# A two-layer decoder trunk on one core: norm and first queries ahead of the values' products, scores with turned sign, two heads' scores in the two halves of the array's rows

## The chip, the core and the metric

The kernel runs on one core of a Trainium2 chip. The time is that of one execution on the device, in microseconds (us). The core has a matrix engine (TensorE, 128 x 128, which multiplies a stationary operand loaded beforehand with a moving one), VectorE, ScalarE, GpSimd, and SyncE (SP), which here only issues DMAs. Every engine works through a queue of its own in order and waits at semaphores for the others. Products land in eight PSUM banks of 128 x 512 floats, which GpSimd can't read.

## What is computed

A trunk of two layers on 512 tokens of width 1024 in float32: a causal pooling mixer with a gated MLP, then sliding-window attention with a gated MLP, and a final norm. The change concerns the attention alone (16 heads of width 64, 4 key/value heads, window 128):

```python
hn = rms_norm(h, norm_mix[i])
qkv = hn @ w_qkv + b_qkv
# blocks of 128 queries against the previous and their own block of keys
scores = einsum('bnqkgd,bnskd->bnkgqs', q, kb) * HEAD_DIM ** -0.5
scores = where(mask, scores - slopes * dist, -inf)
m = maximum(max(scores, axis=-1), sink)
p = exp(scores - m)
denom = sum(p, axis=-1) + exp(sink - m)
o = einsum('bnkgqs,bnskd->bnqkgd', p / denom, vb)
h = h + o @ w_o
```

## The kernel before

Every large product is made of three: each float32 operand is split into a high part (fp32r, written by ScalarE) and a low part (the remainder, a subtraction on VectorE or GpSimd), and `mm3` (lines 82 to 86) adds high x high, high x low and low x high in one bank. `weights` (93 to 100) fetches a 512 KB tile of weights over SP into one of three raw buffers and splits it into one of four pairs of buffers; a fifth tile waits until the first is used up.

Ahead of the attention the last MLP product adds into the residual `h`, and `after0` (367) splits `h` scaled by the norm's weights into `xs1` and adds up the squares on GpSimd. The norm's factor itself is applied to the products afterwards: `stats` (226) sums the squares over the features with eight narrow products and makes the reciprocal root of 4 numbers per partition with 13 small VectorE operations, `spread` (235) turns it into a 128 x 512 tile `rb`.

The attention (lines 382 to 621) runs:

- *Head* (410 to 474): products of the two key tiles (weights 0 and 1), of the values (96 products of 256 columns), `stats`, the product of the first query tile (weights 2), `spread`. Then the key tiles are scaled and get their bias (`ku`), `keys(0)` splits the first key head, `queries(0, ...)` the first two query heads, and the values are evacuated and split into `vh`, `vl`. A key head is kept twice, in the upper and the lower 64 rows, and a query head has its high part in one half of the rows and its low part in the other, so that one full-height product gives high x high plus low x high, and a second one gives the two products with the low part of the keys.
- *Units* (593 to 613): 4 key heads x 4 query blocks. Unit i issues its scores, unit i-2 is transposed, unit i-3 is weighted with the values. `scores` (525) makes eight products of 256 columns, adds slope and distance and takes the maximum on VectorE, turns its sign (`neg`), forms the sinks' term `es`, takes the exponentials with row sums on ScalarE, and scales with the reciprocal of the sum on GpSimd. Between these steps `fill` puts products of the remaining queries (8 steps of three products for each of 7 tiles) and of the output weights, at `RATE` steps a unit, after 16 steps ahead of unit 0.
- *Tail* (614 to 621): the remaining output products and the addition into `h`.

The tile `q` has 8 buffers, two for each of four query tiles. The banks of the scores are a ring `s` of three, those of the projections a ring `pj` of two. The order of instructions on each engine is made by a planner from the program's order and its own estimates of durations; a product may be put between those of another step where it expects a wait.

Of the kernel before, what the change touches and what calls it, by code (L numbers as in the profile page):

```python
# [19 lines left out]
F32 = mybir.dt.float32  # L20
# [3 lines left out]
ALU = mybir.AluOpType  # L24
# [33 lines left out]
def trunk(ctx: ExitStack, tc: tile.TileContext, x_tok, x_t, vecs, w_pool, w_kq, w_v, w_o, w_in, w_out, out_a, out_b):  # L58
# [18 lines left out]
    def bank(tag):  # L77
        rings[tag].append(rings[tag].pop(0))
        return banks[rings[tag][-1]]
# [303 lines left out]
    with tc.tile_pool(name="ap", bufs=2) as ap:  # L383
# [18 lines left out]

        def proj(i, ps, ks=range(NC), w=None):
            w = w or weights(w_kq[i], D, f"kq{i}", G)
            for k in ks:
                mm3(ps, part(w, k), xs1[k], k == 0, k == NC - 1)
            return w


        qps = bank("pj")  # L410
        vps = [bank("s") for a in range(2)]
        ssp = bank("av")
        kps = [bank("t") for c in range(2)]
        kw = [weights(w_kq[i], D, f"kq{i}") for i in range(2)]
        wv = [weights(w_v[:, a * 1024 : (a + 1) * 1024], 1024, f"wv{a}") for a in range(2)]
        for k in range(NC):
            for c in range(2):
                proj(c, kps[c], [k], kw[c])
        for j in range(NT):
            for k in range(NC):  # L420
                xk = tuple(t[:, j * P : (j + 1) * P] for t in xs1[k])
                wk = part(wv[k // 4], k % 4, 256)
                mm3(vps[j // 2][:, (j % 2) * 256 : (j % 2 + 1) * 256], xk, wk, k == 0, k == NC - 1)
        r = norm1.stats(ssp)
        proj(2, qps)
        rb = norm1.spread(bank("s"), r)

        ku = []
        for c in range(2):
            u = ap.tile([P, S], F32, name=f"ku{c}", bufs=1)  # L430
            V.tensor_tensor(u, kps[c], rb, ALU.mult)
            V.tensor_scalar(u, u, col(V_BQKV + 8 + c), None, ALU.add)
            ku.append(u)

        def keys(n):

            src = slice((n % 2) * HD, (n % 2 + 1) * HD)
            dst = slice((1 - n % 2) * HD, (2 - n % 2) * HD)
            u = ku[n // 2]
            kh = ap.tile([P, S], F32R, tag="kh", name=f"kh{n}")  # L440
            kl = ap.tile([P, S], F32R, tag="kl", name=f"kl{n}")
            A.activation(kh[src], u[src], AF.Copy)
            V.tensor_tensor(kl[src], u[src], kh[src].bitcast(F32), ALU.subtract)
            A.activation(kh[dst], u[src], AF.Copy)
            V.tensor_copy(kl[dst], kl[src].bitcast(F32))
            return kh, kl

        def queries(c, ps):

            u = sm.tile([P, S], F32, tag="sq", name=f"q{c}_u")  # L450
            V.tensor_tensor(u, ps, rb, ALU.mult)
            A.activation(u, u, AF.Identity, scale=qs[:, c : c + 1], bias=bqs[:, c : c + 1])
            res = []
            for par in range(2):
                src = slice(par * HD, (par + 1) * HD)
                dst = slice((1 - par) * HD, (2 - par) * HD)
                t = ap.tile([P, S], F32R, tag="q", name=f"q{c}_{par}", bufs=8)
                A.activation(t[src], u[src], AF.Copy)
                V.tensor_tensor(t[dst], u[src], t[src].bitcast(F32), ALU.subtract)  # L459
                res.append(t)  # L460
            return res

        key = {0: keys(0)}
        q = {0: queries(0, qps)}
        for j in range(NT):
# [6 lines left out]
            V.tensor_tensor(dl, v4, dh.bitcast(F32), ALU.subtract)  # L472
        oh = ap.tile([P, NC, S], F32R, name="oh", bufs=1)
# [27 lines left out]
        def work():  # L501

            for c in range(1, NC):
                for _ in fill_q(c):
                    yield 0
# [19 lines left out]
        def scores(n, b):  # L525
# [4 lines left out]
            sink = vec[:, V_SINK + 4 * n : V_SINK + 4 * n + 4]  # L530
            kk = max(b - 1, 0) * P
            sc = []
            for pr in range(2):
                ps = bank("s")
                st = ap.tile([P, 2, 2 * P], F32, tag="sc", name=f"sc{n}{b}{pr}", bufs=6)
                for par in range(2):
                    o = ps[:, par * 256 : par * 256 + 256]
                    qt = q[2 * n + pr][par][:, b * P : (b + 1) * P]
                    for x, kt in enumerate(key[n]):
                        T.matmul(o, lhsT=qt, rhs=kt[:, kk : kk + 256], start=x == 0, stop=x == 1)  # L540
                for par in range(2):
# [3 lines left out]
                        in0=ps[:, par * 256 : par * 256 + w],  # L545
                        in1=dist[:, 2 * P - w :],
                        scale=slopes[4 * n + i],
                        scalar=sink[:, i : i + 1],
                        op0=ALU.add,
                        op1=ALU.max,  # L550
# [3 lines left out]
            V.tensor_scalar(neg, neg, -1.0, None, ALU.mult)  # L554
            V.tensor_tensor(es, neg, sink, ALU.add)
            A.activation(es, es, AF.Exp)
            heads = [sc[i // 2][:, i % 2, :w] for i in range(4)]
            for i, t in enumerate(heads):
                A.activation(t, t, AF.Exp, bias=neg[:, i : i + 1], accum_out=den[:, i : i + 1])  # L559
# [34 lines left out]
        RATE = 3.4  # L594
        fill(2 * NC, 0)
        sc, pt = {}, {}
        for i in range(NU + 3):
            base = 2 * NC + i * RATE
            have = max(i - 3, 0) if i < NU else NU
            if i < NU:  # L600
                n, b = units[i]
                if b == 0:
                    fill((2 * n + 1) * NC, 0)
                sc[i] = scores(n, b)
                if b == 2 and n + 1 < NKV:
                    key[n + 1] = keys(n + 1)
# [159 lines left out]
```

## Time and profile before

| | |
|---|---|
| median of 3 runs | 944.49 us (944.37 to 944.62) |
| profiled execution | 944.47 us, of which the span of the core 942.7 us |
| mean granted TensorE clock | 0.993 of full speed |
| busy share of the span: TensorE, VectorE, ScalarE, GpSimd | 97%, 62%, 45%, 15% |
| attention, from its first to its last product | 390.3 to 569.8 us |

The profile is that of one execution. A group of rows gives the line of the program, the engine, the operation with its operands (names of tiles) and shapes; "idle before" is the time an engine stood still ahead of it, with the operation that ended it. A matmul's duration contains the time until its results have left the array, so that back-to-back products overlap; their rate is read from the distance of their starts. `PEld` is the loading of stationary operands, which overlaps the products. `PEclk` is the granted clock of TensorE in a stretch, 1.00 being 2.4 GHz.

### The profile page before, as it was taken

To read this page: it belongs to the slowest core of one execution; us is meant where nothing else is said; L and a number is where in the kernel's file an instruction comes from. 1 tells how busy PE (TensorE), PEld (TensorE's weight loads), DVE (VectorE), ACT (ScalarE), POOL (GpSimd) and SP (SyncE) were. 2 spreads that over 40 slices of the span, in tenths; PEclk is the share of its full clock that TensorE was granted. 3 is DMA by queue.
4 is the path that set the end of the run, shared out by engine and by line. 5 is a ranking of instruction groups with operands and counts; after the bars stand their busy time and mean duration, and the time that the engine had idled before them with its cause. 6 is when DMAs were issued, how large, how long until landed. Compare 5 with 4: busy or idle time off the path is not lost.

```text
span 942.7 us, 11713 instructions
## 1 busy us (share of the span) xinstructions
PE 919.2 (97%) x4419; PEld 773.1 (82%) x4419; DVE 587.2 (62%) x974; ACT 426.5 (45%) x690; POOL 138.9 (15%) x203
## 2 busy tenths in 40 slices
PE   8999999999999999996999999999999999999997
PEld 7788888888888888885888888888888888888886
DVE  5689775336777654338888581897753367776433
ACT  7565443223444434226877561644432234444432
POOL 9600000000000001442654231000000000000023
PEclk9999999999999999998999999999999999999999
DMA  9133322342322233321101041332223332232312
GB/s 331 64 112 112 111 63 79 98 140 92 112 90 84 75 90 109 112 90 67 46 24 46 1 135 45 112 125 98 65 89 94 133 111 91 90 98 63 92 62 90
DMA packets 28855, 88.13 MB, mean 93 GB/s; under 512 B 3200, under 2 KB 4352, under 8 KB 28800
## 3 DMA queue, kind: packets, MB, share of 16 engines
q1 hardware_dynamic: 28800, 87.40, 28.3%
q8 instruction: 34, 0.56, 0.2%
q14 instruction: 21, 0.17, 0.1%
HBM read 85.29 MB, written 2.10 MB: 93 GB/s over the span
## 4 chain that ended last, share of the span: by engine, by line
PE 90%; DVE 5%; ACT 3%; POOL 1%; issue 1%; ACTq 0%; DVEq 0%; POOLq 0%
PE bank L85 29%; PE bank L84 29%; PE bank L86 29%; PE bank L540 1%; DVE q L459 1%; PE bank L571 1%; ACT sc L559 1%; DVE sc L543 1%; ACT px_h L251 0%; DVE tl L575 0%; DVE vl L472 0%; ACT wi_h L98 0%; PE bank L271 0%; DVE f0x_l L252 0%; PE bank L230 0%
## 5 line engine op out<-in xcount | busy, mean ns | idle before, releaser
L224 POOL TENSOR_TENSOR n_acc<-n_acc,n_sq 128x512 f32<-128x512 f32 (+1 forms) x28 | 39.1, 1397 | 714.2 <-ACT n_sq L215 707.7
L98 ACT ACTIVATE wi_h<-wi_raw 128x1024 fp32r<-128x1024 f32 x88 | 93.0, 1061 | 109.3 <-PE bank L85 102.4
L85 PE MATMUL bank<-f0x_l,wi_h 128*128 128x512 f32 x352 | 137.1, 389 | 0.8 <-DVE f0x_l L252 0.8
L84 PE MATMUL bank<-f0x_h,wi_h 128*128 128x512 f32 x352 | 137.3, 390 | 0.0
L84 PE MATMUL bank<-f1x_h,wi_h 128*128 128x512 f32 x352 | 137.1, 390 | 0.0
L84 PE MATMUL bank<-zh,wo_h 128*128 128x512 f32 (+1 forms) x363 | 137.0, 378 | 0.0
L86 PE MATMUL bank<-f0x_h,wi_l 128*128 128x512 f32 x352 | 137.0, 389 | 0.0
L86 PE MATMUL bank<-f1x_h,wi_l 128*128 128x512 f32 x352 | 137.0, 389 | 0.0
L85 PE MATMUL bank<-f1x_l,wi_h 128*128 128x512 f32 x352 | 136.9, 389 | 0.0
L86 PE MATMUL bank<-zh,wo_l 128*128 128x512 f32 (+1 forms) x363 | 136.6, 376 | 0.0
L85 PE MATMUL bank<-zl,wo_h 128*128 128x512 f32 (+1 forms) x363 | 136.6, 376 | 0.0
L99 DVE TENSOR_TENSOR wi_l<-wi_raw,wi_h 128x1024 fp32r<-128x1024 f32 x84 | 102.8, 1225 | 48.8 <-ACT wi_h L98 36.7
L98 ACT ACTIVATE wo_h<-wo_raw 128x768 fp32r<-128x768 f32 (+1 forms) x70 | 57.5, 822 | 124.0 <-PE bank L85 112.1
L313 DVE TENSOR_TENSOR c_u<-bank,n_rb 128x512 f32<-128x512 f32 x88 | 60.1, 688 | 76.2 <-PE bank L86 76.2
L99 DVE TENSOR_TENSOR wo_l<-wo_raw,wo_h 128x768 fp32r<-128x768 f32 (+1 forms) x66 | 60.4, 915 | 54.4 <-ACT wo_h L98 54.2
L86 PEld LDWEIGHTS bank<-zh,wo_l 128*128 128x128 f32 x363 | 68.3, 188 | 12.5
L84 PEld LDWEIGHTS bank<-zh,wo_h 128*128 128x128 f32 x363 | 68.3, 188 | 12.4
L85 PEld LDWEIGHTS bank<-zl,wo_h 128*128 128x128 f32 x363 | 68.3, 188 | 12.3
L85 PEld LDWEIGHTS bank<-f0x_l,wi_h 128*128 128x128 f32 x352 | 66.1, 188 | 14.7 <-DVE f0x_l L252 1.2
L84 PEld LDWEIGHTS bank<-f0x_h,wi_h 128*128 128x128 f32 x352 | 66.1, 188 | 14.2 <-DVE h L305 0.4
L86 PEld LDWEIGHTS bank<-f1x_h,wi_l 128*128 128x128 f32 x352 | 66.1, 188 | 13.9
L316 ACT ACTIVATE c_t<-c_u,vec 128x512 f32<-128x512 f32 x88 | 70.6, 810 | 15.2 <-DVE c_u L313 14.3
(173 smaller groups left out, 1510.6 us busy)
## 6 DMA issues: line engine op xcount, KB each, us to landing
wi_raw<-w_in SPq DMA_DIRECT2D x88, 512.0 KB, 3.2
wo_raw<-w_out SPq DMA_DIRECT2D x31, 384.0 KB, 3.0
wo_raw<-w_out SPq DMA_DIRECT2D x31, 320.0 KB, 2.9
kq_raw<-w_kq SPq DMA_DIRECT2D x10, 512.0 KB, 3.2
wo_raw<-w_o SPq DMA_DIRECT2D x8, 512.0 KB, 3.3
xt<-x_tok SPq DMA_DIRECT2D x4, 512.0 KB, 5.2
h<-x_t SPq DMA_DIRECT2D x8, 256.0 KB, 7.5
wpool_raw<-w_pool SPq DMA_DIRECT2D x2, 512.0 KB, 8.2
```

Of the source, the lines that this page charges most:

```text
L84: T.matmul(ps, lhsT=wh, rhs=xh, start=start, stop=False, **kw)
L85: T.matmul(ps, lhsT=wh, rhs=xl, start=False, stop=False, **kw)
L86: T.matmul(ps, lhsT=wl, rhs=xh, start=False, stop=stop, **kw)
L98: A.activation(h[:, :n], raw[:, :n], AF.Copy)
L99: (eng or V).tensor_tensor(l[:, :n], raw[:, :n], h[:, :n].bitcast(F32), ALU.subtract)
L224: eng.tensor_tensor(self.acc[:, lo:hi], self.acc[:, lo:hi], sq[:, lo:hi], ALU.add)
L313: V.tensor_tensor(u, ps, rb, ALU.mult)
L316: A.activation(t, u, AF.Identity, bias=col(V_CB + layer * 2 * NF + m), scale=cw[2])
L459: V.tensor_tensor(t[dst], u[src], t[src].bitcast(F32), ALU.subtract)
L540: T.matmul(o, lhsT=qt, rhs=kt[:, kk : kk + 256], start=x == 0, stop=x == 1)
L543: V.tensor_tensor_reduce(out=st[:, par, :w], in0=ps[:, par * 256 : par * 256 + w], in1=dist[:, 2 * P - w :], scale=slopes[4 * n + i], scal ...
L559: A.activation(t, t, AF.Exp, bias=neg[:, i : i + 1], accum_out=den[:, i : i + 1])
```

## The change

The order of the head becomes: keys, `stats`, the product of the first queries (its weights are fetched before those of the values), `spread`, the second half of the value weights, the values, then `ku`, keys, first queries, and, before the values are evacuated, the product of the second queries. The low part of query weights 2 and 3 is made by VectorE instead of GpSimd.

`keys` now splits a whole tile with two key heads once, and four DMAs make a copy with the halves exchanged (`ksh`, `ksl`). `queries` keeps high and low part in two full tiles (three buffers each). `scores` multiplies with the 64 rows of one head alone: for each of two heads in the upper and the lower rows three products, alternating between the halves, each half with a bank of its own. The scores come out with the opposite sign of the bias, so that a minimum gives `neg` at once; the exponentials take a scale of -1, and `es` is formed by GpSimd from `neg` and a sink of turned sign (`nsink`), its exponential behind those of the heads. `RATE` goes from 3.4 to 4, the 16 steps ahead of unit 0 go, and the fill covers query tiles 2 to 7.

```diff
         def proj(i, ps, ks=range(NC), w=None):
-            w = w or weights(w_kq[i], D, f"kq{i}", G)
+            w = w or weights(w_kq[i], D, f"kq{i}", G if i > 3 else V)
...
-        qps = bank("pj")
-        vps = [bank("s") for a in range(2)]
-        ssp = bank("av")
         kps = [bank("t") for c in range(2)]
         kw = [weights(w_kq[i], D, f"kq{i}") for i in range(2)]
-        wv = [weights(w_v[:, a * 1024 : (a + 1) * 1024], 1024, f"wv{a}") for a in range(2)]
+        w0 = weights(w_kq[2], D, "kq2")
+        wv = [weights(w_v[:, :1024], 1024, "wv0")]
         for k in range(NC):
             for c in range(2):
                 proj(c, kps[c], [k], kw[c])
+        r = norm1.stats(bank("av"))
+        qps = bank("pj")
+        proj(2, qps, w=w0)
+        rb = norm1.spread(bank("s"), r)
+        wv.append(weights(w_v[:, 1024:], 1024, "wv1"))
+        vps = [bank("s") for a in range(2)]
         for j in range(NT):
...
-        r = norm1.stats(ssp)
-        proj(2, qps)
-        rb = norm1.spread(bank("s"), r)
...
-            u = ap.tile([P, S], F32, name=f"ku{c}", bufs=1)
+            u = ap.tile([P, S], F32, tag=("th", "tl")[c], name=f"ku{c}")
...
+        def keys(c):
+
+            res = []
+            kh = ap.tile([P, S], F32R, tag="kh", name=f"kh{c}")
+            kl = ap.tile([P, S], F32R, tag="kl", name=f"kl{c}")
+            A.activation(kh, ku[c], AF.Copy)
+            V.tensor_tensor(kl, ku[c], kh.bitcast(F32), ALU.subtract)
+            for t, tag in ((kh, "ksh"), (kl, "ksl")):
+                x = ap.tile([P, S], F32R, tag=tag, name=f"{tag}{c}")
+                for a in range(2):
+                    nc.sync.dma_start(x[a * HD : (a + 1) * HD].bitcast(F32), t[(1 - a) * HD : (2 - a) * HD].bitcast(F32))
+                res.append((t, x))
+            return res
...
+            th = ap.tile([P, S], F32R, tag="qh", name=f"q{c}_h", bufs=3)
+            tl = ap.tile([P, S], F32R, tag="ql", name=f"q{c}_l", bufs=3)
+            A.activation(th, u, AF.Copy)
+            V.tensor_tensor(tl, u, th.bitcast(F32), ALU.subtract)
+            return th, tl
 
         key = {0: keys(0)}
         q = {0: queries(0, qps)}
+        qps = bank("pj")
+        proj(3, qps)
         for j in range(NT):
...
+        q[1] = queries(1, qps)
...
-            for c in range(1, NC):
+            for c in range(2, NC):
...
+            ps = [bank("s") for par in range(2)]
             for pr in range(2):
+                for x, (y, z) in enumerate(((0, 0), (1, 0), (0, 1))):
+                    for par in range(2):
+                        rows = slice(par * HD, (par + 1) * HD)
+                        T.matmul(
+                            ps[par][:, pr * 256 : pr * 256 + 256],
+                            lhsT=q[2 * n + pr][y][rows, b * P : (b + 1) * P],
+                            rhs=key[n // 2][z][(par + n) % 2][rows, kk : kk + 256],
...
-                        scale=slopes[4 * n + i],
+                        scale=-slopes[4 * n + i],
                         scalar=sink[:, i : i + 1],
                         op0=ALU.add,
-                        op1=ALU.max,
+                        op1=ALU.min,
                         accum_out=neg[:, i : i + 1],
                     )
                 sc.append(st)
-            V.tensor_scalar(neg, neg, -1.0, None, ALU.mult)
-            V.tensor_tensor(es, neg, sink, ALU.add)
-            A.activation(es, es, AF.Exp)
+            G.tensor_tensor(es, neg, sink, ALU.subtract)
             heads = [sc[i // 2][:, i % 2, :w] for i in range(4)]
             for i, t in enumerate(heads):
-                A.activation(t, t, AF.Exp, bias=neg[:, i : i + 1], accum_out=den[:, i : i + 1])
+                A.activation(t, t, AF.Exp, bias=neg[:, i : i + 1], scale=-1.0, accum_out=den[:, i : i + 1])
+            A.activation(es, es, AF.Exp)
...
-        RATE = 3.4
-        fill(2 * NC, 0)
+        RATE = 4
         sc, pt = {}, {}
         for i in range(NU + 3):
-            base = 2 * NC + i * RATE
+            base = i * RATE
...
-                    fill((2 * n + 1) * NC, 0)
+                    fill(2 * n * NC, 0)
                 sc[i] = scores(n, b)
-                if b == 2 and n + 1 < NKV:
-                    key[n + 1] = keys(n + 1)
+                if b == 0 and n == 0:
+                    key[1] = keys(1)
```

## Rows read from the trace of the kernel before

**Rows 1.** The page's first part: busy time, share of the span, instructions.
```profile
PE 919.2 (97%) x4419; PEld 773.1 (82%) x4419; DVE 587.2 (62%) x974; ACT 426.5 (45%) x690; POOL 138.9 (15%) x203
```

**Rows 2.** Busy time by stretch of the attention: length, engines, clock, DMA.
```profile
390.30:413.50 23.20, 23.20 (x153) 21.30 (x151) 2.66 (x4) 5.84 (x7) 13.36 (x25) 1.00 0.27 90
413.50:445.70 32.20, 24.32 (x102) 19.30 (x102) 26.63 (x52) 16.38 (x28) 11.42 (x5) 0.89 0.24 81
445.70:538.70 93.00, 88.69 (x564) 78.71 (x563) 73.04 (x244) 68.44 (x208) 44.26 (x69) 0.98 0.08 30
538.70:569.80 31.10, 31.10 (x138) 25.72 (x137) 21.54 (x22) 15.63 (x23) 9.44 (x6) 1.00 0.36 119
```

**Rows 3.** TensorE's waits: who ended them, us in total, times, longest.
```profile
PE bank L540 <- DVE q L459: 5.2, 3, 2.3
PE bank L84 <- DVE q_u L451: 3.3, 1, 3.3
```

**Rows 4.** Timeline of TensorE at unit 0: start, duration, line, operands, idle before.
```profile
435.15 0.28 PE L540 MATMUL bank<-kl,q 128*128 128x256 f32 x1
435.27 0.28 PE L540 MATMUL bank<-kh,q 128*128 128x256 f32 x1
...
440.68 0.58 PE L540 MATMUL bank<-kh,q 128*128 128x256 f32 x1 [2.03 <-DVE q L459]
...
441.70 0.63 PE L85 MATMUL bank<-ax_l,kq_h 128*128 128x512 f32 x1
442.13 0.63 PE L86 MATMUL bank<-ax_h,kq_l 128*128 128x512 f32 x1
```

**Rows 5.** Timelines of GpSimd (POOL) and VectorE (DVE) in the head.
```profile
412.66 4.75 POOL L99 TENSOR_TENSOR kq_l<-kq_raw,kq_h 128x1024 fp32r<-128x1024 f32 x2 [6.20 <-ACT kq_h L98]
434.97 5.11 POOL L99 TENSOR_TENSOR kq_l<-kq_raw,kq_h 128x1024 fp32r<-128x1024 f32 x2 [9.02 <-PE bank L85]
...
415.11 2.32 DVE L193 TENSOR_SCALAR rs_y<-rs_i 128x4 int32<-128x4 int32 x1
417.35 0.16 DVE L194 TENSOR_SCALAR rs_v<-rs_v 128x4 f32<-128x4 f32 x1
...
435.44 5.18 DVE L459 TENSOR_TENSOR q<-q_u,q 64x512 fp32r<-64x512 f32 x2 [1.22 <-ACT q L458]
```

**Rows 6.** Groups by line in the attention: busy us, mean ns, idle before.
```profile
L459 DVE TENSOR_TENSOR q<-q_u,q 64x512 fp32r<-64x512 f32 x16 | 15.5, 972 | 3.5 <-ACT q L458 3.2
L458 ACT ACTIVATE q<-q_u 64x512 fp32r<-64x512 f32 x16 | 10.0, 626 | 0.3
L452 ACT ACTIVATE q_u<-q_u,bqs,qs 128x512 f32<-128x512 f32 x8 | 6.5, 810 | 4.7 <-DVE q_u L451 4.7
L451 DVE TENSOR_TENSOR q_u<-bank,n_rb 128x512 f32<-128x512 f32 x8 | 5.5, 683 | 0.9 <-PE bank L86 0.8
L555 DVE TENSOR_TENSOR es<-neg,vec 128x4 f32<-128x4 f32 x16 | 5.1, 320 | 0.2
L554 DVE TENSOR_SCALAR neg<-neg 128x4 f32<-128x4 f32 x16 | 5.0, 312 | 0.1
L443 DVE TENSOR_TENSOR kl<-ku,kh 64x512 fp32r<-64x512 f32 x4 | 2.8, 708 | 0.1
```

**Rows 7.** Timelines of TensorE around the statistics, and of its weight loads.
```profile
412.72 0.95 PE L230 MATMUL bank<-ones,n_acc 128*128 128x2 f32 x8
413.53 0.47 PE L84 MATMUL bank<-ax_h,kq_h 128*128 128x512 f32 x1
...
413.50 0.19 PEld L84 LDWEIGHTS bank<-ax_h,kq_h 128*128 128x128 f32 x1
```

**Rows 8.** The page's DMA issues: KB each, median us from issue to landing.
```profile
out_a<-o SPq DMA_DIRECT2D x8, 128.0 KB, 1.7
```

**Rows 9.** Timeline of TensorE within unit 12's scores.
```profile
512.82 0.40 PE L84 MATMUL bank<-oh,wo_h 128*128 128x512 f32 x1
513.05 0.40 PE L85 MATMUL bank<-ol,wo_h 128*128 128x512 f32 x1
```

More of the change, by code (lines that the diff above doesn't have):

```diff
@@ L401, in trunk @@
             G.memset(t.bitcast(F32), 0.0)
+        nsink = small(ap, NH, 64, name="nsink", bufs=1)
+        V.tensor_scalar(nsink, vec[:, V_SINK : V_SINK + NH], -1.0, None, ALU.mult)
         def proj(i, ps, ks=range(NC), w=None):
-            w = w or weights(w_kq[i], D, f"kq{i}", G)
+            w = w or weights(w_kq[i], D, f"kq{i}", G if i > 3 else V)
             for k in ks:
@@ L433, in trunk @@
             ku.append(u)
[L435 to L446, printed above, removed]
+        def keys(c):
[10 more added lines that the diff above has]
+            return res
         def queries(c, ps):
@@ L452, in queries @@
             A.activation(u, u, AF.Identity, scale=qs[:, c : c + 1], bias=bqs[:, c : c + 1])
[L453 to L461, printed above, removed]
+            th = ap.tile([P, S], F32R, tag="qh", name=f"q{c}_h", bufs=3)
[3 more added lines that the diff above has]
+            return th, tl
         key = {0: keys(0)}
         q = {0: queries(0, qps)}
+        qps = bank("pj")
+        proj(3, qps)
         for j in range(NT):
@@ L529, in scores @@
             es = small(ap, 4, 16, tag="es", name=f"es{n}{b}", bufs=3)
-            sink = vec[:, V_SINK + 4 * n : V_SINK + 4 * n + 4]
+            sink = nsink[:, 4 * n : 4 * n + 4]
             kk = max(b - 1, 0) * P
             sc = []
+            ps = [bank("s") for par in range(2)]
             for pr in range(2):
-                ps = bank("s")
-                st = ap.tile([P, 2, 2 * P], F32, tag="sc", name=f"sc{n}{b}{pr}", bufs=6)
[L536 to L540, printed above, removed]
+                for x, (y, z) in enumerate(((0, 0), (1, 0), (0, 1))):
[5 more added lines that the diff above has]
+                            rhs=key[n // 2][z][(par + n) % 2][rows, kk : kk + 256],
+                            start=pr == 0 and x == 0,
+                            stop=x == 2,
+                            skip_group_check=True,
+                        )
+            for pr in range(2):
+                st = ap.tile([P, 2, 2 * P], F32, tag="sc", name=f"sc{n}{b}{pr}", bufs=6)
                 for par in range(2):
@@ L544, in scores @@
                         out=st[:, par, :w],
-                        in0=ps[:, par * 256 : par * 256 + w],
+                        in0=ps[par][:, pr * 256 : pr * 256 + w],
                         in1=dist[:, 2 * P - w :],
-                        scale=slopes[4 * n + i],
+                        scale=-slopes[4 * n + i],
                         scalar=sink[:, i : i + 1],
                         op0=ALU.add,
-                        op1=ALU.max,
+                        op1=ALU.min,
                         accum_out=neg[:, i : i + 1],
```

## The prediction

> **What bounds the kernel now.** I read the page first: TensorE is busy for 97% of the span [rows 1], so the kernel can only get faster by giving TensorE less to do or fewer gaps. Then the table by stage, since a mean over stages hides where the gaps are. The attention stage runs from 390.3 to 569.8 us, and I cut it in four [rows 2]. In the first and the last piece TensorE is busy in every microsecond. In the head (413.5 to 445.7, from the norm to the end of unit 0's scores) it is busy 24.32 of 32.20 us: 7.88 us idle, at a mean clock of 0.89. In the units (445.7 to 538.7) it is busy 88.69 of 93.00: 4.31 us idle, clock 0.98. All the rest of the 942.7 us span is dense and untouched, so the change is decided in these two pieces.
>
> The waits of TensorE name who ends the gaps: VectorE's low halves of the queries (5.2 us in 3 waits) and VectorE's first evacuation of a query bank (3.3 us) [rows 3]. The timelines then say why VectorE is late. Its operations with both sides in SBUF get stretched while GpSimd runs a large subtraction: an operation on 4 numbers takes 2.32 us beside GpSimd's 4.75 us, where the next one takes 0.16, and two query subtractions take 5.18 us beside 5.11 us [rows 5], where a key subtraction of the same shape takes 0.71 [rows 6]. And a long wait costs twice: behind the second idle stretch (2.03 us) the 512-column matmuls follow each other at 0.43 us [rows 4] instead of 0.23 [rows 9]; these are the 1.2 and 2.4 GHz levels. From 437.9 to 445.0 some nine 512-column matmuls pay 0.20 each and four 256-column ones 0.09 each, 2.1 us. In the units a clock of 0.98 over 93 us is 1.9 us of lost clock; part of it lies in the idle time, and I take 1.5. So the head holds 7.9 + 2.1 = 10.0 us that is not needed work, and the units hold 4.3 + 1.5 = 5.8 us.
>
> **The head: order.** Now the keys' products are followed by the values' (11.5 us of TensorE), then the norm statistics, the first queries (5.4 us), the spread of the norm, and only then everything VectorE has to do before a score can start. After the change the statistics and first queries come right behind the keys, then the spread, then the values. VectorE's chain (keys scaled and split, first queries split) then lies beside 11.5 us of value products, and the second queries (5.4 us more) still follow. The chain itself is short: five evacuations and splits of full height (keys, key split, queries, query split) at about 0.69 and two shorter bias additions on VectorE, with ScalarE's 0.81 and 0.63 in between [rows 6], under 7 us. The 3.3 us wait goes; the values' own evacuation is late next, and it is needed only when the first weighted product starts, two units into the loop. The weight split of the third and fourth projections moves from GpSimd to VectorE (GpSimd's 4.75 and 5.11 us are two such splits each [rows 5]; VectorE needs about two full-height operations, 1.4 us, for the same). It lies beside the first queries and the values, and takes from the head two of the GpSimd subtractions that block VectorE; those for the fifth projection on stay there.
>
> What is left open in the head: the spread waits for the norm's 13 small operations, 13 x 0.2 = 2.6 us when not blocked, plus two weight splits, against 5.4 us of queries: 0.3 to 1.0 us. The second half of the value weights needs a buffer that the keys hold, and its split may stand behind the norm in VectorE's queue: 0 to 1.8 us. The first scores need the second queries too (one evacuation 0.69, ScalarE 0.81 + 0.63, one subtraction 0.69: 2.8 us after the last product): 0 if other products are put there, 2.8 if not. That is 0.3 to 5.6 us, and if the longest makes the clock fall, 2.1 more. I take 1.5 left of the 10.0, since the order of the kernel before already puts ready products between score products (two output products at 512.82 and 513.05 stand between those of one unit [rows 9]). **Head: -8.5 us, between -9.7 and -2.3.**
>
> **DMAs of the swapped keys.** Each pair of key heads now needs four copies of 128 KB in SBUF, issued on SP. A transfer of that size lands in 1.7 us [rows 8]. They wait for the key split, and on SP's queue the next weight fetches stand behind them. For the first pair both lie beside the value products, ten microseconds ahead of the first score; for the second pair unit 0 issues them and unit 8 needs them. Zero, and if the cover were gone, some 2 to 3 us once.
>
> **The units: VectorE, ScalarE, GpSimd.** Turning the sign drops `neg` and moves `es` to GpSimd: 5.0 + 5.1 us of VectorE, stretched operations included. Queries go from two half-height subtractions (15.5 us in all) to one full one, 8 x 0.69 = 5.5. Keys lose half their subtractions and all the copies between halves [rows 6]. VectorE has 73.0 us of work in the 93 us of units and loses some 18 of it (10 for the two small ones, 7 or so for the queries still to come, 1 or 2 for the keys); ScalarE loses half of its query and key copies. `es` and `neg` average 0.32 and 0.31 us on 4 numbers and queries 0.97 for half a tile, so these operations are among the stretched ones that TensorE ends up waiting behind. So I take 3.0 of the 5.8 us back; all of it would be -5.8. Against it: only three query tiles are kept, where four pairs fitted, and the fill before a key head's first unit stops with the last queries it needs. So at three places the 2.8 us chain has no lead of its own: up to +8.4 if nothing is put there, less the 5.8 that might go: +2.6 for the units as a whole. `es` on GpSimd also stands behind its weight splits of some 2.4 us, and ScalarE's exp of it keeps later copies waiting: inside the same bound. **Units: -3.0, between -5.8 and +2.6.**
>
> **Scores on TensorE.** Now each unit has 8 products of 256 columns with full height, following each other at 0.12 us [rows 4]: 128 x 0.12 = 15.3 us. Afterwards there are 12 per unit with half height, in pairs on the upper and lower rows: 192 products in 96 pairs. No product of half height is in this trace. If a pair takes the time of one product, 96 x 0.12 = 11.5 us, -3.8. If the halves take turns, 192 x 0.12 = 23.0, +7.7; the nearest row for a bare change of weights is the statistics, eight weight loads with 2-column products from 412.72 to 413.53 [rows 7], 0.10 each, and 192 x 0.10 gives +4.1. I take the pair at one slot, as the two halves share no row and write to different banks, which the code takes care of.
>
> Then there is the change between full and half height, twice a unit, 32 times. A boundary between score and projection products costs nothing now; a product of 256 columns takes 0.28 us where the next starts after 0.12 [rows 4], so emptying the array would cost 0.16, and a weight load of 0.19 [rows 7] that can no longer run ahead would make it 0.35. The ends are 0, 5.1 and 11.2 us. I take 0.08, half of emptying, as the next loads can be waiting: 2.6 us. **Scores: -3.8 + 2.6 = -1.2, between -3.8 and +18.9.**
>
> **Sum.** -8.5 - 3.0 - 1.2 = -12.7 us. The profiled execution took 944.47 us, of which 942.7 is the span, and agrees with the median of 944.49. 944.5 - 12.7 = 931.8, which I round to 932.
>
> **Rivals.** *The array empties at every change of height.* 32 x 0.16 = 5.1 instead of 2.6: scores +1.3, the whole 934.3. For it: a product's results come out 0.16 us after its last column [rows 4]; against: boundaries between kinds of full-height products show nothing. The Trainium skill, page "TensorEngine Tiling (Array Packing)", section "Key Properties", has it as a rule that a change of tiling mode drains TensorE; no run here shows one yet.
>
> *The halves take turns* (the change does not do what it says): loading weights is the limit, each half product keeps a slot of 0.10. For it: narrow products with their own weights don't go below 0.10 now, and weight loads are nearly back to back in scores. Against: nothing in the trace separates loading from streaming at 256 columns. Scores become +4.1 + 2.6 = +6.7, the whole 944.5 - 8.5 - 3.0 + 6.7 = 939.7. The Trainium skill, page "TensorE: Matmul & The Clock Gate", section "LDWEIGHTS (loading the stationary operand)", says that loading fewer rows takes no less time; all weights of this trace have full height.
>
> *The queries come late*: with no lead, the three starts of a key head cost what the relief of VectorE gave and more: units +2.6 instead of -3.0, the whole 937.4. For it: the waits for queries are now the largest [rows 3]. Against: VectorE is at 79% of the units now and would be near 60%.
>
> *Slower: change of height with turns.* If both hold, the halves take 0.12 each (+7.7) and each change costs 0.35 (+11.2), then -11.5 + 18.9 = +7.4, 951.9. It decides from 0.12 us a change on if the halves take turns at 0.12 (3.8 us left over 32 changes); with true pairs it would need 0.48 us a change.
>
> **How the numbers follow.** Forecast 0.36, spreading from 925 (all at its best: -9.7 - 5.8 - 3.8 = -19.3) to 937; emptied array 0.22, close to it; turns 0.21; late queries 0.11; slower 0.10. The range of 926 to 943 takes in the first four but for their edges. Faster by over 0.2% means below 942.6 (0.2% is about what can be measured here): 0.56 + 0.18 + 0.10 = 0.84; within it 0.06; slower 0.10.
>
> **What the profile after would show.** Right: value products directly behind the spread, no TensorE gap above 1 us before unit 0, clock 1.00 between 413 and 446; two score products starting within some 0.02 us of each other and a pair each 0.12; `rs_y` at 0.16 us; VectorE near 55 us in the units. Wrong: score products at even distances of 0.10 or more (turns); a gap of 0.2 us or more ahead of and behind each block of scores (change of height); TensorE waiting on `ql` at units 4, 8 and 12 (late queries); a wait for `ksh` or `ksl` (DMAs).

## The result and the profile after

The changed kernel takes 933.99 us (median; 933.92 to 935.64), the kernel before 944.43 beside it: a ratio of 0.9894, with 95% interval 0.9877 to 0.9911, 10.4 us less. The forecast was 932, its range 926 to 943. The profiled execution took 933.92 us, with a span of 932.2.

The page's first part, and busy time by stretch of the attention (columns as in [rows 2]; the stretches are keys; statistics, queries, values and unit 0; the other units; tail):

```profile
PE 919.7 (99%) x4483; PEld 768.3 (82%) x4483; DVE 568.8 (61%) x931; ACT 417.6 (45%) x676; POOL 134.0 (14%) x217
...
390.30:401.20 10.90, 10.90 (x51) 9.03 (x49) 2.78 (x5) 2.88 (x4) 7.73 (x22) 1.00 0.29 96
401.20:430.30 29.10, 28.75 (x184) 25.02 (x183) 17.59 (x38) 12.84 (x18) 9.75 (x4) 1.00 0.44 130
430.30:528.00 97.70, 96.34 (x645) 79.34 (x644) 64.28 (x215) 66.08 (x205) 46.64 (x86) 1.00 0.11 38
528.00:559.30 31.30, 31.30 (x146) 26.13 (x145) 21.81 (x23) 16.11 (x23) 9.42 (x6) 1.00 0.36 118
```

TensorE now idles 0.35 + 1.36 us in the middle two stretches, where it idled 7.88 + 4.31 [rows 2], and its clock is 1.00 in all of them. Idle time and clock alone would promise more than the 10.4 us that came; the units, from the end of unit 0's scores to the tail, hold 96.3 us of busy TensorE in place of 88.7. Only 2.4 us of that is work: by the slots given below, this stretch has 86.3 us of products instead of 83.9, since 33 more products of 512 columns lie in it and 12 fewer of 256. The other 5 us are explained below. Its waits in the attention:

```profile
PE bank L544 <- ACT q_h L461: 1.2, 1, 1.2
PE bank L544 <- DVE q_l L462: 0.4, 1, 0.4
```

In place of 8.5 us for queries in [rows 3], 1.6 are left. In the head, values follow directly on the spread, and the norm's small operation is short again (TensorE, then VectorE):

```profile
407.34 0.39 PE L86 MATMUL bank<-ax_h,kq_l 128*128 128x512 f32 x1
407.57 1.05 PE L241 MATMUL bank<-n_d,ones 128*128 128x128 f32 x8
408.37 0.36 PE L84 MATMUL bank<-wv_h,ax_h 128*128 128x256 f32 x1
...
404.58 0.16 DVE L193 TENSOR_SCALAR rs_y<-rs_i 128x4 int32<-128x4 int32 x1
```

`rs_y` took 2.32 us in [rows 5]. Now one unit's scores on TensorE:

```profile
459.13 0.40 PE L86 MATMUL bank<-ax_h,kq_l 128*128 128x512 f32 x1
459.45 0.38 PE L544 MATMUL bank<-ksh,q_h 64*128 64x256 f32 x1
459.46 0.38 PE L544 MATMUL bank<-kh,q_h 64*128 64x256 f32 x1
459.68 0.28 PE L544 MATMUL bank<-ksh,q_l 64*128 64x256 f32 x1
459.68 0.28 PE L544 MATMUL bank<-kh,q_l 64*128 64x256 f32 x1
459.80 0.28 PE L544 MATMUL bank<-ksl,q_h 64*128 64x256 f32 x1
...
460.15 0.28 PE L544 MATMUL bank<-kl,q_h 64*128 64x256 f32 x1
460.36 0.50 PE L84 MATMUL bank<-ax_h,kq_h 128*128 128x512 f32 x1
460.70 0.40 PE L85 MATMUL bank<-ax_l,kq_h 128*128 128x512 f32 x1
```

The halves start together (0.00 to 0.01 us apart) and a pair takes 0.12: the pairing works. But the block has seams. Ahead of it a 512-column product keeps 0.32 us to itself instead of 0.23; the first pair keeps 0.22 instead of 0.12; the last pair keeps 0.21; and the first full-height product behind keeps 0.34. That is 0.10 + 0.10 at each of the two changes of height, 0.40 a block, and the idle column of these rows is empty. From the product ahead (459.13) to the second one behind (460.70) are 1.57 us; less two products of 0.227, a block of twelve halves costs 1.12 us. Eight full-height products of before cost 8 x 0.12 = 0.96.

**Where the time went.** "Idle before" counts a product as running until its results have left, so I added up the distances of TensorE's starts over the attention instead, and took off what each product takes in a dense stretch (0.227 us for 512 columns, 0.12 for 256, half of that for a half-height one). The head is counted here to the first score of unit 1, at 445.7 us before and 430.6 after; unit 0's own scores end at 441.3 before, where the prediction puts their end at 445.7. Before, the head had 11.3 us beyond the dense slots, and the units 9.4. After, the head has 1.9 and the units 11.5. The scores of after stand in 25 blocks, not 16 (the planner cuts those of units 0, 4, 8 and 12 into 6 + 2 + 4, since the second queries of a key head come later, and those of unit 15 in two): 25 x 0.40 = 10.0 us, 3 of the blocks in the head. What is left for waits is 11.3 to 0.7 in the head and 9.4 to 2.7 in the units (0.5 of it in unit 1, where the halves don't run as pairs; its rows stand at the end):

| | before | after | difference | predicted (bounds) |
|---|---|---|---|---|
| waits and lost clock, head | 11.3 | 0.7 | -10.6 | -8.5 (-9.7 to -2.3) |
| waits and lost clock, units | 9.4 | 2.7 | -6.7 | -3.0 (-5.8 to +2.6) |
| scores: slots saved and seams | 0 | -3.8 + 10.0 | +6.2 | -1.2 (-3.8 to +18.9) |
| sum | | | -11.1 | -12.7 |

The distance from the first key product to the first of the next MLP fell from 179.5 to 168.5 us, by 11.0; the rest of the span is 0.5 longer, and the profiled executions differ by 10.55. So a sum that came out 2 us off holds three terms that were off by 2.1, 3.7 and 7.4. The experiments ask whether these three really are separate.

### The profile page after: what moved, and what is told of

Read it like the earlier page. It is cut to its first block, busy times and chain, and to the rows that moved or that the text cites. A ratio compares the mean times of both kernels' runs of the same rounds, so it can differ in the third digit from the quotient of the medians.

```text
span 932.2 us, 11779 instructions
## 1 busy us (share of the span) xinstructions
PE 919.7 (99%) x4483; PEld 768.3 (82%) x4483; DVE 568.8 (61%) x931; ACT 417.6 (45%) x676; POOL 134.0 (14%) x217
## 4 chain that ended last, share of the span: by engine, by line
PE 93%; ACT 3%; DVE 2%; POOL 2%; issue 1%; ACTq 0%; POOLq 0%; DVEq 0%
PE bank L84 30%; PE bank L85 30%; PE bank L86 30%; PE bank L544 1%; PE bank L583 1%; ACT sc L570 1%; ACT px_h L251 0%; DVE tl L587 0%; PE bank L241 0%; PE bank L271 0%; ACT wi_h L98 0%; DVE f0x_l L252 0%; DVE q_l L462 0%; PE bank L230 0%; POOL kq_l L99 0%
```

## The experiments

Each kernel of before that ran beside them took 943.98, 944.36 or 944.11 (medians). "Full height" is the keys, queries and scores of before.

**Undoing the half heights, and then the sign.** In e1, `keys`, `queries` and the products of `scores` are those of before, all else is the change. In e2 the sign is that of before as well (`neg` turned and `es` formed on VectorE, its exponential ahead of the others), so that only the head's new order and the new fill remain. (`scores` also still writes both banks' products ahead of VectorE's work on them, as in the change; so it does in e5 and in all the other runs but e11.)

```diff
--- e1: the changed kernel with scores of full height
-            ps = [bank("s") for par in range(2)]
+            ps = []
             for pr in range(2):
-                        T.matmul(ps[par][:, pr * 256 : pr * 256 + 256],
-                            lhsT=q[2 * n + pr][y][rows, b * P : (b + 1) * P], ...
+                ps.append(bank("s"))
+                    for x, kt in enumerate(key[n]):
+                        T.matmul(o, lhsT=qt, rhs=kt[:, kk : kk + 256], start=x == 0, stop=x == 1)
--- e2: e1 without the turned sign
-                        op1=ALU.min,
+                        op1=ALU.max,
-            G.tensor_tensor(es, neg, sink, ALU.subtract)
+            V.tensor_scalar(neg, neg, -1.0, None, ALU.mult)
+            V.tensor_tensor(es, neg, sink, ALU.add)
+            A.activation(es, es, AF.Exp)
```

> The changed kernel, but with the scores, the split of keys and queries and the query buffers of the kernel before: eight full-height products a unit, no change of height. Order of the head, turned sign, fill and rate stay as changed. Theory (a change of height costs 0.20 us, as the starts around the score blocks of the changed kernel show: 25 blocks x 0.40 = 10.0 us, against 3.8 us saved by pairs and 0.5 lost where unit 1 is not paired): the changed kernel minus 6.7, plus up to 3 for VectorE's and ScalarE's larger share: 927 to 930. Rival (the pairs are what the change gained, changes of height are nearly free): 938 to 941.

> As the run with full-height scores, and the sign, neg and es as in the kernel before: the kernel before with the new order of the head and the new fill alone. Theory (head worth about 10, units some 3 of which the smaller VectorE load is the cause): 930 to 933. Rival A (the units' stalls went because the head hands over without delay, not because of the sign): as the run with the sign, within 0.7. Rival B (the sign is worth its 10 us of VectorE in large part): 934 or more.

e1 took 931.32 us (931.08 to 932.59; ratio 0.987, 0.985 to 0.9889): 2.7 *less* than the changed kernel, between the two cases that were expected and near the theory. The two halves of the array's rows lose time. e2 took 939.30 (937.6 to 940.66; ratio 0.9958, 0.9937 to 0.9979): with the sign of before 8.0 of e1's gain are gone, as in rival B. TensorE's longest wait in the attention of e2, then of e1:

```profile
PE bank L547 <- DVE q L462: 5.6, 4, 1.9
...
PE bank L549 <- DVE q L464: 3.4, 2, 2.9
```

Both wait for VectorE's low halves of the queries, at the starts of key heads: the rival "the queries come late" is real here, and heavier without the turned sign. One of e1's waits in its place:

```profile
448.52 0.39 PE L85 MATMUL bank<-ax_l,kq_h 128*128 128x512 f32 x1
451.76 0.39 PE L549 MATMUL bank<-kh,q 128*128 128x256 f32 x1 [2.86 <-DVE q L464]
```

The idle column says 2.86 us; the start came 3.24 us behind the one before it, 3.01 more than a dense stretch has. That difference (0.16 a gap) is why idle time undercounts.

**Is the head's gain hidden in e2?** The head's new order alone, with the fill of before (8 steps ahead of unit 0, then 3.4 a unit; all else as before):

```diff
--- e5: before, with the new order of the head; the fill of before
-        RATE = 4
+        RATE = 3.4
+        fill(NC, 0)
...
-            base = i * RATE
+            base = NC + i * RATE
```

> The kernel before with the new order of the head alone (statistics, first queries and spread ahead of the values; second queries ahead of the loop; low parts of query weights 2 and 3 on VectorE); sign, full-height scores, and the fill with its lead of some eight steps and 3.4 steps a unit as before. The head-only run with the new fill came to 939.3 and its trace waits 5.6 us for queries at the starts of key heads. Theory (the head is worth its 8.5, the new fill alone gives 3 to 4 back because the queries of a key head have no lead): 935 to 936. Rival (the head is worth only 5): 939 again.

932.79 us (932.69 to 932.87; ratio 0.9888, 0.9862 to 0.9915). The head's order alone is worth 11.6 us: more than the whole change and more than either case expected. By the starts, its head has 0.2 us of waits left, its units 8.1, and the stretches show which half of the attention moved:

```profile
401.20:435.00 33.80, 33.80 (x208) 30.38 (x207) 23.52 (x52) 18.31 (x26) 12.17 (x5) 1.00 0.28 94
435.00:528.00 93.00, 88.28 (x568) 77.88 (x567) 74.90 (x248) 70.56 (x213) 43.74 (x69) 1.00 0.11 35
```

No idle time in the head, and units as before: 88.28 of 93.00 against 88.69 [rows 2]. From e5 to e2 only the fill differs (no steps ahead of unit 0, 4 a unit), and it costs 6.5 us.

**The turned sign alone.** e11 is the kernel before with the sign turned, e9 is e5 with the sign turned (`es` on VectorE there).

```diff
--- e11: before with the sign turned (e9: the same on e5, with V for G)
-                        scale=slopes[4 * n + i],
+                        scale=-slopes[4 * n + i],
-                        op1=ALU.max,
+                        op1=ALU.min,
-            V.tensor_scalar(neg, neg, -1.0, None, ALU.mult)
-            V.tensor_tensor(es, neg, sink, ALU.add)
-            A.activation(es, es, AF.Exp)
+            G.tensor_tensor(es, neg, sink, ALU.subtract)
```

> The kernel before with the turned sign alone, es on GpSimd as in the change; old head, old fill, full-height scores. The prediction gave the units' relief 3.0 us, all edits together. Theory (part of the 5.8 us of waits in the units go with neg and es): 940.5 to 943. Rival (es on GpSimd costs what neg gives): 944 to 945.

> The new order of the head, the fill with its old lead and rate, full-height scores, the turned sign with es on VectorE. The head alone with this fill came to 932.8, and 5.9 us of waits in the units are left there, the same as in the kernel before. Theory (the sign takes work from VectorE at just these waits): 927 to 929.5, below the 928.9 of the best run so far or beside it. Rival (the sign only repairs what the new fill breaks): 932 to 933.

e11: 944.01 us (941.07 to 944.64; ratio 0.9996, 0.9982 to 1.001). e9: 932.95 (932.89 to 932.97; ratio 0.9878, 0.9863 to 0.9893) beside e5's 932.79. Both rivals held: with the old fill the sign is worth nothing. Yet VectorE is relieved; the units of e11, in the same stretch as [rows 2]:

```profile
445.70:538.70 93.00, 87.34 (x567) 77.66 (x566) 67.99 (x215) 68.82 (x208) 45.03 (x84) 1.00 0.09 30
```

VectorE has 68.0 us of work instead of 73.0, and TensorE is no busier. In e9 TensorE's longest wait is for another tile of VectorE's (in e5 that wait was 1.9 us in two):

```profile
PE bank L85 <- DVE tl L585: 4.4, 3, 1.8
```

**Who should form `es`, and is the lead missed?** e7 is e1 with `es` on VectorE; e10 is the changed kernel with the same edit; e6 is e1 with 8 steps ahead of unit 0 and a rate of 3.5.

```diff
--- e7 (on e1), e10 (on the changed kernel)
-            G.tensor_tensor(es, neg, sink, ALU.subtract)
+            V.tensor_tensor(es, neg, sink, ALU.subtract)
--- e6 (on e1)
-        RATE = 4
+        RATE = 3.5
+        fill(NC, 0)
...
-            base = i * RATE
+            base = NC + i * RATE
```

> The changed kernel with full-height scores, as in the first run, but with a lead of eight steps ahead of unit 0 and 3.5 steps a unit, so that queries are ready when a key head starts: 19 score blocks instead of 23. Theory (the 3.4 us that TensorE waits for queries there go): 927.5 to 929. Rival (the waits move to later units): 931.

> As the first run with full-height scores (931.3), but es is formed by VectorE instead of GpSimd; neg stays away. Separates the two halves of the turned sign, which together were worth 8.0 us (939.3 to 931.3). Theory A (VectorE stands still with es behind GpSimd's long subtractions, so moving it is most of the gain): 935 to 938. Theory B (what counts is neg, one operation less between the scores and the exponentials): 931 to 933.

> The changed kernel with es on VectorE instead of GpSimd and nothing else. With full-height scores this gave 931.3 to 928.9. Theory (an operation on GpSimd between scores and row sums waits behind its splits and scalings, and the exp of es and what follows it wait with it): 931 to 932.5. Rival (TensorE hardly waits in the changed kernel, 1.8 us in all, so there is nothing to gain): 933.5 to 934.5.

e6: 933.42 us (932.56 to 934.18; ratio 0.9894, 0.9872 to 0.9916), 2.1 above e1 and worse than both of its cases. e7: **928.91** (928.74 to 929.22; ratio 0.9847, 0.9816 to 0.9878), 2.4 below e1, below both of its cases and the fastest kernel of all. e10: 933.79 (933.74 to 935.39; ratio 0.9891, 0.9876 to 0.9906), no change from 933.99, as its rival said. The waits, e6 then e7:

```profile
PE bank L85 <- DVE tl L585: 3.9, 4, 2.4
PE bank L549 <- DVE q L464: 0.5, 1, 0.5
...
PE bank L549 <- DVE q L464: 0.9, 1, 0.9
```

With a lead, the wait for queries falls to 0.5 us but the transposed scores (`tl`) come late instead, presumably because fewer steps are left between the units. With `es` on VectorE 0.9 us of the one and 0.2 of the other are left. The same stretch in e2, e1 and e7:

```profile
430.00:533.00 103.00, 96.40 (x583) 84.90 (x583) 76.85 (x254) 72.43 (x216) 43.00 (x70) 0.95 0.11 37
...
430.00:533.00 103.00, 99.08 (x621) 87.70 (x620) 71.82 (x227) 75.91 (x219) 47.80 (x86) 1.00 0.11 37
...
430.00:533.00 103.00, 101.51 (x629) 89.39 (x628) 78.10 (x246) 77.67 (x221) 42.95 (x70) 1.00 0.12 39
```

TensorE's busy time climbs from 96.4 to 99.1 and 101.5, and in e2, with the longest waits, the clock is 0.95. That clock is a large part of the differences. By the starts, e2's attention has 15.0 us beyond the dense slots, 8.6 of them at its waits; e1 has 6.6 and 4.3, e5 8.4 and 5.6. The rest, 6.4 us against 2.2 and 2.8, are products that follow each other more slowly (in e2 at 0.43 us for 512 columns from 508.0 to 509.3, behind the wait that ends at 504.89). So about half of what the new fill costs from e5 to e2, and of what the sign gives from e2 to e1, is clock.

In this window the faster kernel gets more work done; over the whole attention VectorE has 121.6 us in e2, 111.8 in e1 and 116.2 in e7. It still works more in e7 than in e1, and e7 is faster: what counts is not its sum, but how soon the step that TensorE waits for is done. GpSimd has 43 us in e2 and e7 and 47.8 in e1. At e1's longest wait (the 2.86 us above) the traces show what held up the queries: their two subtractions lie beside two of GpSimd's weight splits and take 3.46 us. In e7 the same two are done before the split begins and take 1.40 (e1, then e7):

```profile
446.46 4.70 POOL L99 TENSOR_TENSOR kq_l<-kq_raw,kq_h 128x1024 fp32r<-128x1024 f32 x2 [0.18 <-ACT kq_h L98]
448.97 3.46 DVE L464 TENSOR_TENSOR q<-q_u,q 64x512 fp32r<-64x512 f32 x2 [2.08 <-ACT q L463]
...
448.08 1.40 DVE L464 TENSOR_TENSOR q<-q_u,q 64x512 fp32r<-64x512 f32 x2
450.78 2.40 POOL L99 TENSOR_TENSOR kq_l<-kq_raw,kq_h 128x1024 fp32r<-128x1024 f32 x1 [3.92 <-ACT kq_h L98]
```

`es` itself does not come late on GpSimd: from a unit's last minimum to the sum that needs `es` it is 1.4 us in e1 and 1.5 in e7, on average over the 16 units. So at this wait the move of `es` costs time through a different placing of the weight splits; that it is the move that makes the planner place them so is an inference, and for the other waits the causes were not separated.

**The price of a change of height, and of taking turns.** e4 adds a full-height product of two columns, with zeros, in the middle of each unit's scores; e3 writes the products of the upper half ahead of those of the lower; in e8 both heads of a pair use the upper rows, so that the second head's scores are made from the first head's rows.

```diff
--- e4: one narrow product of full height in each unit's scores
+                if pr:
+                    T.matmul(ps[0][:, 256:258], lhsT=nil, rhs=nil[:, :2], start=False, stop=False, ...)
--- e3: half by half in the program's order
-                for x, (y, z) in enumerate(((0, 0), (1, 0), (0, 1))):
-                    for par in range(2):
+                for par in range(2):
+                    for x, (y, z) in enumerate(((0, 0), (1, 0), (0, 1))):
--- e8: both products of a pair on the same rows
-                        rows = slice(par * HD, (par + 1) * HD)
+                        rows = slice(0, HD)
```

> The changed kernel with the three products of the upper half first, then the three of the lower half, in each half unit: the same 192 products. Theory (products of different halves that stand side by side run at the same time, 0.12 a pair): of six products only two neighbours overlap, five slots instead of three, 32 x 2 x 0.12 = +7.7 us, 941 to 942. Rival (the halves take turns, the equal starts in the trace are an artefact): no change, 934.

> The changed kernel with one full-height product of 2 columns, all zeros, in the middle of each unit's scores: 37 score blocks instead of 25, so 24 more changes of height, and 16 products of about 0.10 us. Theory (0.20 us a change): 24 x 0.20 + 1.6 = +6.4 us, 940.4. Rival A (a change is free): +1.6, 935.6. Rival B (the 0.08 of the prediction): +3.5, 937.5.

> The changed kernel with both products of each pair on the upper 64 rows: the scores of the second head of a pair are made from the first one's rows, everything else stands, count and order included. Theory (pairs run at the same time only because they use different rows): 96 more slots of 0.12, +11.5 us less what the waits absorb, 944 to 946. Rival (the pair is fast for another reason, or half products are short): 934.

e3 took 934.4 us and says nothing on pairing: the planner put the products back in alternating order. e4 took 938.13, 3.7 above e3 on the same chip (one execution each). Twelve of its 16 narrow products landed inside a block; one of them:

```profile
454.19 0.28 PE L548 MATMUL bank<-kl,q_h 64*128 64x256 f32 x1
454.40 0.27 PE L544 MATMUL bank<-nil 128*128 128x2 f32 x1
454.60 0.38 PE L548 MATMUL bank<-ksh,q_h 64*128 64x256 f32 x1
...
454.82 0.28 PE L548 MATMUL bank<-ksh,q_l 64*128 64x256 f32 x1
```

From the pair ahead to the second pair behind are 0.63 us, where two pairs take 0.23: 0.40 for the narrow product and its two changes together, and 12 x 0.40 = 4.8 against 3.7 in the time. If the narrow product keeps the 0.10 that such a product takes in [rows 7], 0.15 are left for each change; only if it hides within the changes is it 0.20. The theory's +6.4 counted the narrow products beside changes of 0.20 each. By its time alone e4 is nearest to rival B (937.5, a change at 0.08); the starts rule that out, since 0.08 a change would make 0.10 + 2 x 0.08 = 0.26 of the 0.40. e8 took 942.77 (one execution), 8.8 above the changed kernel, a little less than expected. Its block:

```profile
467.71 0.38 PE L544 MATMUL bank<-ksh,q_h 64*128 64x256 f32 x1
467.94 0.28 PE L544 MATMUL bank<-kh,q_h 64*128 64x256 f32 x1
468.06 0.28 PE L544 MATMUL bank<-ksh,q_l 64*128 64x256 f32 x1
...
469.13 0.28 PE L544 MATMUL bank<-kl,q_h 64*128 64x256 f32 x1
469.34 0.50 PE L84 MATMUL bank<-ax_h,kq_h 128*128 128x512 f32 x1
```

On the same rows each product keeps 0.12 us for itself, and the block takes 1.63 from its first start to the product behind it, against 0.91 (459.45 to 460.36) in the changed kernel. So two products run at once only because they use different rows.

**The weight splits on GpSimd.** e12 is the changed kernel with the low part of query weights 3 on GpSimd again; weights 2 are fetched by another line and keep VectorE:

```diff
-            w = w or weights(w_kq[i], D, f"kq{i}", G if i > 3 else V)
+            w = w or weights(w_kq[i], D, f"kq{i}", G)
```

> The changed kernel with the low parts of query weights 3 (the second queries; those of weights 2 are fetched with the keys) on GpSimd again, as before. Theory (GpSimd's 2.4 us subtraction holds up VectorE's norm and key operations, but the values' 11.5 us cover it now): 933.5 to 935. Rival (the blocked norm delays the spread, which nothing covers): 936 to 937.

934.69 us (934.61 to 935.15; ratio 0.9897, 0.9883 to 0.9912): 0.7 above the changed kernel's median, though within the scatter of its runs, and 0.9 above e10 on the same chip. GpSimd's split and the norm's operation beside it:

```profile
402.70 3.11 POOL L99 TENSOR_TENSOR kq_l<-kq_raw,kq_h 128x1024 fp32r<-128x1024 f32 x1 [3.73 <-ACT kq_h L98]
...
403.48 2.36 DVE L192 TENSOR_SCALAR rs_i<-rs_v 128x4 int32<-128x4 int32 x1
```

A small operation of the norm is stretched again, as in [rows 5] (`rs_i` here, just ahead of `rs_y`), and the spread waits 0.4 us for the norm; the new order hides the rest.

## Why the prediction was right, and where its steps were wrong

The time lies in the forecast's range, 2 us from its centre. The ladder shows that the likeliest case was right in what it said of the head and wrong in what it said of the scores; that the sum came out so near is luck:

| step | us | step's worth |
|---|---|---|
| before | 944.4 | |
| new order of the head, fill of before (e5) | 932.8 | -11.6 |
| and the new fill (e2) | 939.3 | +6.5 |
| and the turned sign (e1) | 931.3 | -8.0 |
| and half heights (the change) | 934.0 | +2.7 |

A step's worth holds for this order of the steps. With the turned sign in place (`es` on VectorE) the new fill is a gain of 4.0 us (e9's 932.95 to e7's 928.91), where without it it is a loss of 6.5.

**The head (-8.5, measured -10.6 in the changed kernel, -11.6 alone): right in mechanism, too small.** Values behind the spread, VectorE's chain beside them, clock 1.00, `rs_y` at 0.16: all as said. The mis-sized term is "7.9 idle + 2.1 clock = 10.0". By starts it was 11.3, of which idle gaps make 8.7 (four gaps of 0.5, 3.4, 2.4 and 2.3): each is 0.16 to 0.3 longer than the idle column says, and the slow products cost the rest. The 1.5 left over was 0.7.

**The weight splits: right, worth little.** e12 prices one of the two, that of weights 3, at some 0.7 us, hardly more than the scatter; no run has that of weights 2 back on GpSimd.

**DMAs at zero: right.** Copies of the keys landed in 2.8 and 2.9 us (medians), not 1.7, and TensorE never waited for them:

```profile
ksh<-kh SPq DMA_DIRECT2D x4, 128.0 KB, 2.8
ksl<-kl SPq DMA_DIRECT2D x4, 128.0 KB, 2.9
```

The last were issued by 418.3, and the first score starts at 425.5.

**The units (-3.0): a wrong reason.** The prediction took VectorE's relief as a gain on the order of before. e11 and e9 show that this alone is worth nothing. In the ladder the relief is large (-8.0), but it pays back the loss that the new fill brings (+6.5), a rival that got 0.11 and was to cost +2.6 - (-3.0) = 5.6: its size was nearly right, and that it was cured by another part of the same change was not seen. In the changed kernel the queries still hold up TensorE for 1.6 us in two places. VectorE's work fell to 64.28 us in 97.70, not to the 55 of 93 that was named.

**The scores (-1.2): the step that failed.** The pair at one slot was right (-3.8; e8 shows what it would be otherwise), so "the halves take turns" falls, and "slower" with it. The change of height was taken at 0.08 x 32 = 2.6. It is 0.20 x 50 = 10.0: wrong in the price, which lies above the 0.16 of the emptied array, and in the count, since a planner that cuts a block adds two changes for each cut. The sign named for it, a gap of 0.2 us or more ahead of and behind each block, would have missed it: the cost stands in the distances of the starts, with no idle time. "The array empties at every change of height" was the right rival in kind, and its 934.3 is the measured time by accident: it had 5.1 in place of 10.0. The Trainium skill, page "TensorEngine Tiling (Array Packing)", section "Key Properties", has the rule that a change of tiling mode drains TensorE, and that tiles otherwise work in parallel. The trace agrees with the second, and with the first in that each change costs time, 0.20 us beside a pair's 0.12; that the array empties in it, no run shows.

**Why these errors cancelled.** The seams (+6.2 with the saved slots) are mostly TensorE's own time, yet half heights cost only +2.7 from e1. The products of e1 had 6.6 us of waits in the whole attention, by starts; the changed kernel has 0.7 + 2.7. So 3.2 us of the seams were made up for by waits that e1 had and the changed kernel has not. One way to this is that a slower TensorE gives VectorE time, and e8 shows that it happens: its edit adds 96 x 0.12 = 11.5 us to TensorE and leaves the instructions of the other engines as they are, the time rises by 8.8, and none of the changed kernel's waits is left. The other way is that half heights also take work off VectorE (from 430 to 533 us it has 71.8 us in e1 and 64.8 in the changed kernel). How the 3.2 us divide between the two, no run shows. In e10 `es` on VectorE buys nothing, while in e7 it buys 2.4; that little wait was left to remove in the changed kernel fits this, but is argued.

What stays open: what a change of height costs beside a very short product (0.15 to 0.20 us), what placed the weight splits of e1 and e7 differently, and why the units of before keep 8 to 9 us of waits and slower products under every kind of relief with the old fill (e5, e9, e11).

## What to carry to other kernels

Price a packed form by its seams as well as its slots: with 0.20 us a change between products of this size, twelve half-height products in six pairs (1.12 us) lose to eight full-height ones (0.96); by these numbers two units' scores in one block would be the first to win (an estimate: 12 x 0.12 + 0.40 = 1.84 against 1.92). Relief of an engine is worth what the step that ends a wait gains, so test each part of a change on the order that it will run in: the sign was worth 0 on one fill and 8 us on another, about half of them clock, and the best kernel (928.91) takes the new head, the new fill and the sign, and leaves the half heights and the move of `es` out. Count a matrix engine's gaps by the starts of its products, not by its idle column.

## What the runs showed of the hardware

- **A change between full and half height costs 0.20 us**, at either side of a block, between 512- or 256-column products of full height and 256-column pairs. A 2-column product of full height inside a block costs 0.40 with its two changes. The weight loads show part of it. Those of both halves start together, and the first of a block is not pulled ahead of the products (it starts with its product at 459.45, where the next starts 0.12 ahead of its own, at 459.68):

```profile
459.45 0.18 PEld L544 LDWEIGHTS bank<-ksh,q_h 64*128 64x128 f32 x1 [0.36 <-issue]
459.45 0.18 PEld L544 LDWEIGHTS bank<-kh,q_h 64*128 64x128 f32 x1
459.56 0.19 PEld L544 LDWEIGHTS bank<-ksh,q_l 64*128 64x128 f32 x1
```

- **A load of 64 rows takes 0.18 to 0.19 us**, as one of 128 [rows 7]; two on different rows that start together at 459.45 take 0.18 each.
- **A pair shares a slot only when both halves are ready.** In unit 1 a half started alone (the lower half's bank is the third of a ring of three, an inference from the program's order), and the block took 1.21 us from first to last start instead of 0.70. The lower half's first product comes 0.51 us behind the upper's:

```profile
430.64 0.39 PE L544 MATMUL bank<-kh,q_h 64*128 64x256 f32 x1
430.86 0.28 PE L544 MATMUL bank<-kh,q_l 64*128 64x256 f32 x1
...
431.15 0.38 PE L544 MATMUL bank<-ksh,q_h 64*128 64x256 f32 x1
```

- **A copy of 128 KB within SBUF landed in 2.8 to 2.9 us**, where copies of the same size to `out_a` land in 1.7 [rows 8].
